# Attention outputs from stationary values and moving probabilities, two key groups in the two halves of a PSUM bank

## The chip, the core and the metric

The kernel runs on one core of a Trainium2 chip. A core has a matrix engine (TensorE, in the profile PE for matmuls and PEld for its weight loads), a vector engine (VectorE, DVE), an engine for pointwise functions (ScalarE, ACT), GpSimd (POOL) and a queue engine (SP) that here only issues transfers. Each works through its own instructions in a fixed order and waits on semaphores for the others. TensorE multiplies a stationary operand, loaded as weights, with a moving operand that streams past it, and writes into PSUM, whose banks hold 512 fp32 columns on 128 partitions. The metric is the time of one execution on the device in microseconds, the median of three runs. "Before" and "after" are the two versions of the kernel.

## What is computed

Two decoder layers on 256 tokens of width 2048. Each layer projects the normalised input into gating and attention parts, evaluates both, projects back, and adds a feed-forward part. The change is in the attention:

```python
q = rms_norm(q.reshape(b, nb, BLOCK, N_KV_HEADS, GROUP, HEAD_DIM), q_norm_g)   # 16 heads of 64
k = rms_norm(k.reshape(b, nb, BLOCK, N_KV_HEADS, HEAD_DIM), k_norm_g)          # 4 key groups
kb, vb = band(k), band(v)                    # previous and own block of 128 keys
scores = einsum('bnqkgd,bnskd->bnkgqs', q, kb) / sqrt(HEAD_DIM)
scores = where(valid, scores + bias, -1e30)  # causal window of 128 keys, bias per head and distance
probs = softmax(concatenate([scores, sink], -1), -1)[..., :-1]   # one extra logit per head
out_b = einsum('bnkgqs,bnskd->bnqkgd', probs, vb)
...
mixed = concatenate([rms_norm(out_a, out_norm_a), rms_norm(out_b, out_norm_b)], -1)
x = x + mixed @ w_out
x = x + (silu(h2 @ w_gate) * (h2 @ w_up)) @ w_down
```

All inputs and the output are float32. Four query heads share one key group. There are two query blocks of 128 tokens (t = 0 and 1); block 0 has 128 keys, block 1 has 256.

## The kernel before

**Units.** Every large product goes through weights of 256 x 512 fp32, one transfer each (`raw`). `split2` splits them into a high part `wh` (a cast on ScalarE, L99) and a low part `wl` (a subtraction on VectorE, L100), both fp32r; the activations are split the same way (`aT`, `hT`, with a high and a low half). `mm3` (L137 to L140) then makes three matmuls of 512 columns for one product. A unit is one such weight tile with its 12 large matmuls for the two token blocks (`unit`). Five buffers of `wh` and `wl` let the splits run ahead of TensorE by up to five units. In this text units are numbered from the start of a layer, and "behind unit n" is said of the place in TensorE's order.

**Order.** `later(delay, fn)` puts a step so many units ahead, and `tick` emits what is due after a unit. So the attention of a layer is strewn among the units of the input projection: `in_block(6)` (keys and values, units 0 to 7), `in_block(4)` and `in_block(5)` (queries), then four blocks for the gating part. The framework then fixes each engine's order, mostly as emitted, and picks free buffer slots.

**Attention.** `kv_norm` writes the projected keys and values to `zkv` and the normalised, transposed keys to `kT`; `q_norm` scales the queries per head (sum of squares, then a power -0.5 on GpSimd, L186) and transposes them to `qT`. For each key group g and query block t, `attend` computes the scores of four heads with 64-row matmuls, the even and odd heads on the two halves of the rows (L357, into `ps_s`); VectorE adds the bias (L365) and takes the maximum (L370); `nm` is its negative with the sink; ScalarE takes one exponential per head with the sum as a by-product (`den`, L378); VectorE makes `rden`, the reciprocal of the sum with the sink. Three units after `attend` comes `turn`: four transposes of probabilities on TensorE (L392) and a copy to `pt` (L393), twice for t = 1. Then `weigh`: for each head and key block one matmul with the 128 x 128 probabilities stationary and 64 columns of values moving (L399, into `ps_v`), and a multiplication by `rden` into `ob` (L408). When both blocks are done, `attend_end` sums the squares on ScalarE (L215), transposes the outputs (L208) and splits them with the gain of the norm into `pairs_b` (L198, L199). At the end `finish_rms` adds the partial sums to the norm's factor `rstd_b`, which `add_part` applies after the output projection.

**PSUM.** Eight banks: five for accumulators (`acc`), two (`dacc`), one (`sm`). `small_ps` hands them out in turn to the small products. The pool `spt` has four buffers for `s` and `pt`; the pool `big` has eight for `kT`, `qT`, `zkv`, `bias`, `wm` and others.

Of the kernel before, what the change touches and what calls it, by code (L numbers as in the profile page):

```python
# [12 lines left out]
F32 = mybir.dt.float32  # L13
# [3 lines left out]
ALU = mybir.AluOpType  # L17
# [28 lines left out]
)  # L46
ACTS = 6
HOLD = 2
VEC = 1.14
VEC_P = 0.6  # L50
MM = 0.227
# [16 lines left out]
def trunk(ctx, tc, x, xt, w_in, w_out, w_gate, w_up, w_down, sgu_w, sgu_g, consts,  # L68
# [49 lines left out]
    def later(delay, fn):  # L118
        pending.append((clock[0] + delay, next(serial), fn))
# [13 lines left out]
    def small_ps(shape, name):  # L133
        pool, tag = ((pm, "sm"), (pd, "dacc"), (pa, "acc"), (pd, "dacc"))[next(turns) % 4]
        return pool.tile(shape, F32, tag=tag, name=name)
# [33 lines left out]
        nc.tensor.matmul(heat, junk[:, :P], junk, start=i == 0, stop=i == WARM - 1)  # L169
    mhalf = cp.tile([P, 16], F32, tag="mhalf", name="mhalf")  # L170
    nc.vector.memset(mhalf, -0.5)
    tab = cp.tile([P, 16], F32, tag="tab", name="tab")
    nc.scalar.copy(tab, mhalf)
    ident = cp.tile([P, P], F32, tag="ident", name="ident")
# [2 lines left out]
    def small(shape, name):  # L177
        return sp.tile(shape, F32, tag=name, name=name)
# [15 lines left out]
    def split_gain(ps, lay, col, tag, spare=False):  # L194
        pair = pair_tile(tag, spare)
        for j in range(2):
            g = cst[:, lay, col + j : col + j + 1]
            nc.scalar.activation(pair[:, 0, j, :], ps[:, j, :], AF.Copy, scale=g)  # L198
            nc.vector.scalar_tensor_tensor(  # L199
                pair[:, 1, j, :], ps[:, j, :], g, f(pair[:, 0, j, :]), ALU.mult, ALU.subtract  # L200
            )
        return pair

    def transpose_pair(blocks, ps=None):
        ps = small_ps([P, 2, SEQ], "ps_t") if ps is None else ps
        for j in range(2):
            for t in range(NTOK):
                nc.tensor.transpose(  # L208
                    ps[:, j, t * P : (t + 1) * P], blocks[t][:, j * P : (j + 1) * P], ident
                )  # L210
        return ps

    def sum_sq(dst, src):
        void = zp.tile([P, NB], BF16, tag="z", name="void")
        nc.scalar.activation(void[:, : src.free_size()], src, AF.Square, accum_out=dst)  # L215
# [15 lines left out]
    def bc(a, n):  # L231
        return a.unsqueeze(2).to_broadcast([P, a.shape[1], n])
# [42 lines left out]
    for lay in range(L):  # L275
# [14 lines left out]
        def kv_norm(acc, lay=lay, layer=layer, zkv=zkv, kT=kT):  # L290
            kd = []
            zz = ap.tile([P, NTOK, NB], F32, tag="big", name="zkv", bufs=8)
            for t in range(NTOK):
                z = zz[:, t]
                nc.scalar.activation(z, acc[t], AF.Copy, scale=layer["rstd1"][t])
                zkv.append(z)
# [12 lines left out]

            for c in range(2):  # L310
                later(5 + c, lambda c=c: to_T(c))
# [22 lines left out]
            for c in range(2):  # L334
                later(5 + c, lambda c=c: to_T(c))

        ssb = [small([P, NKV], "ss4") for t in range(NTOK)]
        ob = {}
        bias = {}
        pairs_b = [None] * NKV  # L340

# [2 lines left out]
            nc.gpsimd.dma_start(bt, rdram[g * GRP : (g + 1) * GRP].rearrange("h q k -> q h k"))  # L344
            bias[g] = bt

        def attend(g, t, zkv=zkv, kT=kT, qT=qT, ob=ob, bias=bias, layer=layer):
            nkb = t + 1
            nk = nkb * P
            k0 = SEQ - nk  # L350
            nsink = layer["nsink"]
            s = ap.tile([P, GRP, nk], F32, tag="spt", name="s", bufs=4)
            halves = [small_ps([P, 2, nk], "ps_s") for r in range(2)]
            for i in range(2):
                for r in range(2):
                    h = g * GRP + 2 * i + r
                    nc.tensor.matmul(  # L357
                        halves[r][:, i, :],
                        qT[h // 8][HD * r : HD * r + HD, (h % 8) // 2, t * P : (t + 1) * P],
                        kT[HD * r : HD * r + HD, g, :nk],  # L360
                        start=True,
                        stop=True,
                    )
            for r in range(2):
                nc.vector.scalar_tensor_tensor(  # L365
                    s[:, r::2, :], halves[r], 1.0 / math.sqrt(HD), bias[g][:, r::2, k0:],
                    ALU.mult, ALU.add,
                )
            m = small([P, GRP], "m")
            nc.vector.tensor_reduce(m, s, AX.X, ALU.max)  # L370
            hs = slice(g * GRP, (g + 1) * GRP)
            nm = small([P, GRP], "nm")
            nc.vector.scalar_tensor_tensor(nm, m, -1.0, nsink[:, hs], ALU.mult, ALU.min)
            es = small([P, GRP], "es")
            nc.vector.tensor_tensor(es, nm, nsink[:, hs], ALU.subtract)
            den = small([P, GRP], "den")
            for i in range(GRP):
                nc.scalar.activation(  # L378
                    s[:, i, :], s[:, i, :], AF.Exp, bias=nm[:, i : i + 1],
                    accum_out=den[:, i : i + 1],  # L380
                )
            nc.scalar.activation(es, es, AF.Exp)
            rden = small([P, GRP], "rden")
            nc.vector.tensor_tensor(rden, den, es, ALU.add)
            nc.vector.reciprocal(rden, rden)
            pt = ap.tile([P, GRP * nkb, P], F32, tag="spt", name="pt", bufs=4)

            def turn(c):
                pst = small_ps([P, GRP, P], "ps_p")
                s4 = s.rearrange("p h (b k) -> p (h b) k", k=P)  # L390
                for i in range(GRP):
                    nc.tensor.transpose(pst[:, i, :], s4[:, c * GRP + i, :], ident)  # L392
                nc.vector.tensor_copy(pt[:, c * GRP : (c + 1) * GRP, :], pst)  # L393

            def weigh():
                pv = small_ps([P, GRP, HD], "ps_v")
                for i in range(GRP):
                    for b in range(nkb):
                        nc.tensor.matmul(  # L399
                            pv[:, i, :],  # L400
                            pt[:, i * nkb + b, :],
                            zkv[b][:, (NKV + g) * HD : (NKV + g + 1) * HD],
                            start=b == 0,
                            stop=b == nkb - 1,
                        )
                ob[g, t] = zp.tile([P, GRP * HD], F32, tag="z", name="ob")
                o3 = ob[g, t].rearrange("p (h d) -> p h d", d=HD)
                nc.vector.tensor_tensor(o3, pv, bc(rden, HD), ALU.mult)  # L408

            for c in range(nkb):  # L410
                later(3 + c, lambda c=c: turn(c))
            later(5 + t, weigh)

        def attend_end(g, lay=lay, ob=ob, ssb=ssb, pairs_b=pairs_b):
            for t in range(NTOK):
                sum_sq(ssb[t][:, g : g + 1], ob[g, t])
            ps = transpose_pair([ob[g, t] for t in range(NTOK)])
            pairs_b[g] = split_gain(ps, lay, C_GB + 2 * g, "aT", g >= 2)

        gate = {}  # L420

# [103 lines left out]
        acc = in_block(4)  # L525
        load_bias(0)
        q_norm(0, acc)
        for g in range(NKV):
            at = 6 + (27 * g) // 4
            later(at, lambda g=g: attend(g, 0))  # L530
            at += 2
            later(at, lambda g=g: attend(g, 1))
            if g + 1 < NKV:
                later(at, lambda g=g: load_bias(g + 1))
# [258 lines left out]
    return w.reshape(l, k // (4 * P), 2, 2, P, n // NB, NB).transpose(0, 5, 1, 3, 4, 2, 6)  # L793


def _cols(g):
    return g.reshape(-1, P).T

# [60 lines left out]
```

## Time and profile before

| | |
|---|---|
| Median of 3 runs | 1944.8 us (1944.8 to 1944.86) |
| Profiled execution | 1945.16 us, span of the trace 1943.5 us |
| TensorE busy | 1933.4 us, 99% of the span, 8894 matmul passes |
| VectorE, ScalarE, GpSimd busy | 1699.4 us (87%), 1151.3 us (59%), 127.1 us (7%) |
| Granted TensorE clock | 1.00 |

A row of the groups reads: line, engine, operation, output<-inputs, shape, count, then busy time and mean duration (ns) of one, then the engine's idle time before them and what ended it. A row of the timeline reads: start and duration in us, engine, line, operation, count; durations of matmuls overlap, so the distance of two starts is the price. A row of the waits reads: who waited for whom, microseconds in total, times, the longest. A plain fp32 matmul appears as two passes, a large fp32r one and a transpose as one.

### The profile page before, as it was taken

Reading aid. Unit: us, or ns where it says so; the run is one execution under the profiler, and the core shown is the slowest. Engines: PE = TensorE matmul, PEld = TensorE weight load, DVE = VectorE, ACT = ScalarE, POOL = GpSimd, SP = SyncE. Lnnn points to the kernel's source line nnn. Section 1 sums busy time; section 2 is a strip of 40 time slices with the busy share of each in tenths; the row PEclk is TensorE's granted clock in tenths of the full one; section 3 lists DMA queues with packets and bytes.
Section 4 is the critical chain, followed back from the end, with each engine's and each line's share of the span. In section 5 each row is a group of like instructions: output and inputs, shape, how many; then the busy total and the mean of one; then the engine's idle time right before and its main releaser. Section 6 shows DMA issues by size and latency. Waiting matters only on the chain.

```text
span 1943.5 us, 24615 instructions
## 1 busy us (share of the span) xinstructions
PE 1933.4 (99%) x8894; PEld 1588.5 (82%) x8894; DVE 1699.4 (87%) x1909; ACT 1151.3 (59%) x1455; POOL 127.1 (7%) x137
## 2 busy tenths in 40 slices
PE   9999999999999999999999999999999999999998
PEld 7788888888888888888888888888888888888887
DVE  6787689999999999999767876899999999999995
ACT  7465566666565665665555565666666566665662
POOL 1210001000000000000002100000000000000000
PEclk9999999999999999999999999999999999999999
DMA  8854557768668667767655445577677678768773
GB/s 322 266 174 152 184 170 233 223 226 266 216 215 268 219 229 246 221 226 247 206 194 191 158 163 182 176 247 219 222 243 234 215 244 240 237 217 245 240 239 120
DMA packets 119707, 424.43 MB, mean 218 GB/s; under 512 B 13168, under 2 KB 15344, under 8 KB 119584
## 3 DMA queue, kind: packets, MB, share of 16 engines
q1 hardware_dynamic: 106928, 377.57, 54.6%
q0 software_dynamic: 12512, 45.19, 12.5%
q8 instruction: 70, 1.15, 0.2%
q14 instruction: 53, 0.43, 0.1%
q10 hardware_dynamic: 144, 0.08, 0.0%
HBM read 420.66 MB, written 4.23 MB: 219 GB/s over the span
## 4 chain that ended last, share of the span: by engine, by line
PE 94%; DVE 3%; issue 1%; ACT 1%; DMA 1%; SPq 0%; ACTq 0%; DVEq 0%
PE m L140 11%; PE m L139 11%; PE m L138 11%; PE acc L138 10%; PE acc L140 10%; PE acc L139 10%; PE dacc L138 9%; PE dacc L139 9%; PE dacc L140 9%; DVE wl L100 2%; PE ps_v L399 1%; PE ps_f L208 1%; ACT wh L99 1%; PE ps_s L357 1%; PE ps_t L208 1%
## 5 line engine op out<-in xcount | busy, mean ns | idle before, releaser
L99 ACT CAST wh<-raw 128x1024 fp32r<-128x1024 f32 (+1 forms) x778 | 799.7, 1049 | 607.3 <-DVE raw L636 200.5
L100 DVE TENSOR_TENSOR wl<-raw,wh 128x1024 fp32r<-128x1024 f32 (+1 forms) x778 | 925.4, 1217 | 128.2 <-ACT wh L99 121.1
L138 PE MATMUL m<-wh,ext 128*128 128x512 f32 x576 | 225.7, 392 | 0.0
L138 PE MATMUL dacc<-wh,aT 128*128 128x512 f32 x576 | 225.0, 392 | 0.3
L139 PE MATMUL dacc<-wl,aT 128*128 128x512 f32 x576 | 225.1, 391 | 0.0
L139 PE MATMUL m<-wl,ext 128*128 128x512 f32 x576 | 224.6, 390 | 0.0
L140 PE MATMUL dacc<-wh,aT 128*128 128x512 f32 x576 | 224.5, 390 | 0.0
L140 PE MATMUL m<-wh,ext 128*128 128x512 f32 x576 | 224.3, 389 | 0.0
L100 DVE TENSOR_TENSOR wl<-t,wh 128x1024 fp32r<-128x1024 f32 x144 | 175.2, 1219 | 21.8 <-ACT wh L99 18.1
L99 ACT CAST wh<-t 128x1024 fp32r<-128x1024 f32 x144 | 151.4, 1052 | 57.5 <-PE dacc L140 40.0
L138 PE MATMUL acc<-wh,hT 128*128 128x512 f32 x448 | 180.3, 404 | 0.5 <-ACT wh L99 0.5
L139 PE MATMUL acc<-wl,hT 128*128 128x512 f32 x448 | 175.3, 391 | 0.8 <-DVE wl L100 0.7
L140 PE MATMUL acc<-wh,hT 128*128 128x512 f32 x448 | 175.3, 391 | 0.0
L138 PE MATMUL m<-wh,hT 128*128 128x512 f32 x432 | 168.5, 390 | 0.3 <-ACT wh L99 0.3
L140 PE MATMUL m<-wh,hT 128*128 128x512 f32 x432 | 168.1, 389 | 0.0
L139 PE MATMUL m<-wl,hT 128*128 128x512 f32 x432 | 168.1, 389 | 0.0
L138 PE MATMUL acc<-wh,aT 128*128 128x512 f32 x384 | 151.7, 395 | 0.0
L140 PE MATMUL acc<-wh,aT 128*128 128x512 f32 x384 | 149.9, 390 | 0.0
L139 PE MATMUL acc<-wl,aT 128*128 128x512 f32 x384 | 149.7, 390 | 0.0
L644 POOL DMA_DIRECT2D t<-in_w_gate_dram x72 | 61.5, 854 | 1327.3 <-DVE wl L100 828.5
L138 PEld LDWEIGHTS dacc<-wh,aT 128*128 128x128 f32 x576 | 108.1, 188 | 24.0 <-DVE xres L725 1.6
L139 PEld LDWEIGHTS dacc<-wl,aT 128*128 128x128 f32 x576 | 108.2, 188 | 23.9 <-DVE wl L100 2.2
(142 smaller groups left out, 2832.9 us busy)
## 6 DMA issues: line engine op xcount, KB each, us to landing
raw<-in_w_gate_dram SPq DMA_DIRECT2D x176, 512.0 KB, 5.3
raw<-in_w_up_dram SPq DMA_DIRECT2D x176, 512.0 KB, 4.5
raw<-in_w_down_dram SPq DMA_DIRECT2D x176, 512.0 KB, 4.9
raw<-in_w_in_dram SPq DMA_DIRECT2D x108, 512.0 KB, 4.3
t<-in_w_gate_dram POOLq DMA_DIRECT2D x72, 512.0 KB, 6.3
raw<-in_w_out_dram SPq DMA_DIRECT2D x64, 512.0 KB, 3.2
bias<-rdram POOLq DMA_DIRECT2D x8, 512.0 KB, 5.1
raw<-in_w_in_dram SPq DMA_DIRECT2D x8, 256.0 KB, 5.6
```

The source lines that it names most:

```text
L99: nc.scalar.copy(wh[:, j : j + step, :], src)
L100: nc.vector.tensor_tensor(wl[:, j : j + step, :], src, f(wh[:, j : j + step, :]), ALU.subtract)
L138: nc.tensor.matmul(acc, ah, wh, start=first, stop=False, **more)
L139: nc.tensor.matmul(acc, ah, wl, start=False, stop=False, **more)
L140: nc.tensor.matmul(acc, al, wh, start=False, stop=last, **more)
L208: nc.tensor.transpose(ps[:, j, t * P : (t + 1) * P], blocks[t][:, j * P : (j + 1) * P], ident)
L357: nc.tensor.matmul(halves[r][:, i, :], qT[h // 8][HD * r : HD * r + HD, (h % 8) // 2, t * P : (t + 1) * P], kT[HD * r : HD * r + HD, g, :n ...
L399: nc.tensor.matmul(pv[:, i, :], pt[:, i * nkb + b, :], zkv[b][:, (NKV + g) * HD : (NKV + g + 1) * HD], start=b == 0, stop=b == nkb - 1,)
L644: nc.gpsimd.dma_start(t2, w_gate[lay, b, i, 1], accum_op=ALU.add)
```

## The change

Two key groups (2G and 2G+1) and one query block now make one unit of attention (G, t) with eight heads, four per layer. The probabilities are scaled by `rden` on ScalarE right after the exponentials. `turn(b)` transposes one key block for both groups, eight transposes. In `weigh(b)` the values (64 columns, from `vhl`, a copy of the value half of `zkv`) are stationary and 512 columns of probabilities (four heads of 128 queries) move; the first group writes partitions 0 to 63 and the second 64 to 127 of the accumulator `ov`. So the outputs stand with the head's elements on the partitions, which is how the output projection takes them: they are not transposed any more. `leave` squares them, adds up over heads on VectorE, and splits them with the gain into `pairs_b`. `sum_b` adds over partitions with two small matmuls against a column of ones. The rows of `w_out` and the gain `out_norm_b` are reordered on the way in to match (`_paired`). `UNITS` says at which delay the four units come, `LAG` how many units later their first turn.

```diff
+LAG = {(0, 0): 4, (0, 1): 4, (1, 0): 4, (1, 1): 5}
+UNITS = {(0, 0): 6, (0, 1): 11, (1, 0): 19, (1, 1): 24}
...
-        zkv = []
+        vhl = ap.tile([P, NTOK, NKV * HD], F32, tag="big", name="vhl", bufs=8)
...
+                v = z[:, NKV * HD :]
+                nc.scalar.copy(vhl[:, t], v)
...
-        def attend(g, t, zkv=zkv, kT=kT, qT=qT, ob=ob, bias=bias, layer=layer):
+        def attend(G, t, kT=kT, qT=qT, vhl=vhl, ov=ov, bias=bias, layer=layer):
...
+            ss = []
+            for g in (2 * G, 2 * G + 1):
+                s = ap.tile([P, GRP, nk], F32, tag="spt", name="s", bufs=4)
+                halves = [small_ps([P, 2, nk], "ps_s") for r in range(2)]
...
+            for i in range(2 * GRP):
+                nc.scalar.activation(
+                    ss[i // GRP][:, i % GRP, :], ss[i // GRP][:, i % GRP, :], AF.Copy,
+                    scale=rden[:, i : i + 1],
+                )
+            pts = {}
+
+            def turn(b):
+                for k in range(2):
+                    pst = small_ps([P, GRP, P], "ps_p")
+                    for i in range(GRP):
+                        nc.tensor.transpose(pst[:, i, :], ss[k][:, i, b * P : (b + 1) * P], ident)
+                    pt = ap.tile([P, GRP * P], F32, tag="spt", name="pt", bufs=4)
+                    nc.vector.tensor_copy(pt, pst.rearrange("p h q -> p (h q)"))
+                    pts[b, k] = pt
+
+            def weigh(b):
+                if b == 0:
+                    ov[G, t] = pa.tile([P, GRP * P], F32, tag="acc", name="ov")
+                for k in range(2):
+                    g = 2 * G + k
+                    nc.tensor.matmul(
+                        ov[G, t][HD * k : HD * k + HD, :],
+                        vhl[:, b, g * HD : (g + 1) * HD],
+                        pts[b, k],
+                        start=b == 0,
+                        stop=b == nkb - 1,
+                        skip_group_check=True,
+                    )
+                if b == nkb - 1:
+                    leave(G, t)
+
+            for b in range(nkb):
+                later(LAG[G, t] + 3 * b, lambda b=b: turn(b))
+                later(LAG[G, t] + 2 + 3 * b, lambda b=b: weigh(b))
...
-        def attend_end(g, lay=lay, ob=ob, ssb=ssb, pairs_b=pairs_b):
...
+        def leave(G, t, lay=lay, ov=ov, sqs=sqs, pairs_b=pairs_b):
+            o = ov[G, t].rearrange("p (h q) -> p h q", q=P)
+            sq = zp.tile([P, GRP, P], F32, tag="z", name="sq")
+            nc.scalar.activation(sq, o, AF.Square)
+            nc.vector.tensor_reduce(
+                sqs[:, 2 * G + t, :], sq.rearrange("p h q -> p q h"), AX.X, ALU.add
+            )
+            for i in range(GRP):
...
+                nc.scalar.activation(dst[:, 0], o[:, i], AF.Copy, scale=g)
+                nc.vector.scalar_tensor_tensor(
+                    dst[:, 1], o[:, i], g, f(dst[:, 0]), ALU.mult, ALU.subtract
+                )
+
+        def sum_b(t, sqs=sqs):
+            ps = small_ps([P, 1], "ps_q")
+            for G in range(2):
+                nc.tensor.matmul(ps, sqs[:, 2 * G + t, :], ones, start=G == 0, stop=G == 1)
+            return inv_rms(ps, 1, SW)
...
-            later(at + 8, lambda g=g: attend_end(g))
+        later(1, lambda: load_bias(1))
+        for (G, t), at in UNITS.items():
+            later(at, lambda G=G, t=t: attend(G, t))
+        for g in (2, 3):
+            later(UNITS[0, 1] + g - 1, lambda g=g: load_bias(g))
...
-        rstd_b = [finish_rms(ssb[t], SW) for t in range(NTOK)]
+        rstd_b = [sum_b(t) for t in range(NTOK)]
```

More of the change, by code (lines that the diff above doesn't have):

```diff
@@ L171, in trunk @@
     nc.vector.memset(mhalf, -0.5)
+    ones = cp.tile([P, 1], F32, tag="ones", name="ones")
+    nc.vector.memset(ones, 1.0)
     tab = cp.tile([P, 16], F32, tag="tab", name="tab")
@@ L335, in q_norm @@
                 later(5 + c, lambda c=c: to_T(c))
-        ssb = [small([P, NKV], "ss4") for t in range(NTOK)]
-        ob = {}
+        ov = {}
+        sqs = zp.tile([P, 2 * NTOK, P], F32, tag="z", name="sqs")
         bias = {}
@@ L377, in attend @@
-            for i in range(GRP):
+            den = small([P, 2 * GRP], "den")
+            for i in range(2 * GRP):
                 nc.scalar.activation(
-                    s[:, i, :], s[:, i, :], AF.Exp, bias=nm[:, i : i + 1],
-                    accum_out=den[:, i : i + 1],
+                    ss[i // GRP][:, i % GRP, :], ss[i // GRP][:, i % GRP, :], AF.Exp,
+                    bias=nm[:, i : i + 1], accum_out=den[:, i : i + 1],
                 )
             nc.scalar.activation(es, es, AF.Exp)
-            rden = small([P, GRP], "rden")
+            rden = small([P, 2 * GRP], "rden")
@@ L384, in attend @@
             nc.vector.tensor_tensor(rden, den, es, ALU.add)
             nc.vector.reciprocal(rden, rden)
[L386 to L408, printed above, removed]
@@ L410, in attend @@
-            for c in range(nkb):
-                later(3 + c, lambda c=c: turn(c))
-            later(5 + t, weigh)
-        def attend_end(g, lay=lay, ob=ob, ssb=ssb, pairs_b=pairs_b):
[L415 to L418, printed above, removed]
+            for i in range(2 * GRP):
+                nc.scalar.activation(
+                    ss[i // GRP][:, i % GRP, :], ss[i // GRP][:, i % GRP, :], AF.Copy,
+                    scale=rden[:, i : i + 1],
+                )
@@ L813 @@
                     _cols(a["out_norm_a"][l]),
[L814 removed]
+                    _cols(_paired(a["out_norm_b"][l])),
                     a["sgu_b"][l].T,
```

64 lines of the change are left out of this document (32 added, 32 removed).

## The prediction

> **What bounds the kernel now.** I read the page first, then the waits of TensorE, then its stretches and its timeline around the attention.
>
> ```profile
> span 1943.5 us, 24615 instructions
> ...
> PE 1933.4 (99%) x8894; PEld 1588.5 (82%) x8894; DVE 1699.4 (87%) x1909; ACT 1151.3 (59%) x1455; POOL 127.1 (7%) x137
> ...
> PE 94%; DVE 3%; issue 1%; ACT 1%; DMA 1%; SPq 0%; ACTq 0%; DVEq 0%
> ```
> ```profile
> PE heat L169 <- DVE mhalf L171: 1.5, 1, 1.5
> PE acc L139 <- DVE wl L100: 0.7, 2, 0.5
> ```
> ```profile
> 1026.70:1174.90 148.20, 148.20 (x793) 122.65 (x792) 110.83 (x190) 84.70 (x170) 23.42 (x21) 1.00 0.51 173
> ```
>
> TensorE is busy 99% of the span, and the chain that ended last is 94% TensorE. The second fence is the waits of TensorE, longest first: the longest is at the start, the next 0.7 us in two pieces. The third is layer 1's attention stretch (busy us of PE, PEld, DVE, ACT, POOL, then clock): TensorE is busy all 148.2 us at full clock, VectorE 110.8 and ScalarE 84.7. So this kernel takes as long as the instructions on TensorE, one behind the other: a TensorE instruction removed shortens it at full price, one added lengthens it, and work elsewhere is free until TensorE must wait for it. Two sums are wanted: TensorE's time, and new waits.
>
> **The change on TensorE.** The timeline gives the price of each kind, as the distance between starts (the durations overlap):
>
> ```profile
> 37.81 1.03 PE L258 MATMUL ps_r<-oneh,relb 32*16 32x512 f32 x2
> 38.76 0.50 PE L138 MATMUL acc<-wh,hT 128*128 128x512 f32 x1
> ...
> 69.00 0.39 PE L139 MATMUL acc<-wl,hT 128*128 128x512 f32 x1
> ...
> 71.72 0.39 PE L139 MATMUL acc<-wl,hT 128*128 128x512 f32 x1
> ...
> 79.03 1.14 PE L357 MATMUL ps_s<-kT,qT 64*128 64x256 f32 x8
> 80.10 0.50 PE L138 MATMUL acc<-wh,hT 128*128 128x512 f32 x1
> 80.43 0.40 PE L139 MATMUL acc<-wl,hT 128*128 128x512 f32 x1
> ...
> 93.02 0.71 PE L357 MATMUL ps_s<-kT,qT 64*128 64x128 f32 x8
> 93.67 0.66 PE L392 MATMUL ps_p<-ident,s 128*128 128x128 f32 x4
> ...
> 109.53 0.60 PE L208 MATMUL ps_t<-ident,ob 128*128 128x128 f32 x4
> 109.88 0.48 PE L138 MATMUL acc<-wh,hT 128*128 128x512 f32 x1
> ...
> 123.54 1.89 PE L399 MATMUL ps_v<-zkv,pt 128*128 128x64 f32 x16
> 125.24 0.48 PE L138 MATMUL acc<-wh,hT 128*128 128x512 f32 x1
> 125.56 0.39 PE L139 MATMUL acc<-wl,hT 128*128 128x512 f32 x1
> ```
>
> - A unit of 12 large matmuls: 71.72 - 69.00 = 2.72 us, 0.227 each.
> - A plain fp32 matmul is two passes (x8 for 4 calls). A pass with 512 moving columns: (38.76 - 37.81) / 2 = 0.475, part of which is the change of shape; I take 0.44. By columns, 256 then cost 0.22.
> - Score group, 8 passes of 256 columns: 1.07 us, and the second large matmul behind it comes 0.33 instead of 0.227 later: 1.17. Eight passes one behind the other would be 1.76; so the two row halves (64 of 128 rows each) run side by side, 4 x 0.22 = 0.88, and 0.3 is for going into and out of halves. The group of 128 columns, 0.65 to the transposes behind it, says the same: 4 x 0.11 and 0.2 on the way in.
> - Weighted sum of one query block: 16 passes in 1.70, 0.106 each, and 0.09 behind.
> - Four transposes of outputs: 0.35 and 0.09 behind, 0.44.
>
> Removed over both layers: 192 passes L399 x 0.106 = 20.4, with some 0.7 behind the longer groups; 8 groups of output transposes x 0.44 = 3.5; score groups become 8 instead of 16 (two key groups back to back), so 8 entries into halves x 0.3 = 2.4; in layer 0 the first score group is scattered over three places among large matmuls that were late (the 0.7 above), now it stands after its inputs: about 1.3. Together 28.3. Score passes and the 96 transposes of probabilities stay as many.
>
> Added: 12 calls of weigh, each two matmuls (two passes) of 512 columns, into partitions 0-63 and 64-127 of one bank. The trace has no matmul in column halves. If the halves run side by side as the row halves do: 2 x 0.44 + 0.3 = 1.18, 14.2 in all. One behind the other: 4 x 0.44 + 0.3 = 2.06, 24.7. I take the first, the nearest row being L357, also two halves of the array in fp32. Then the sums of squares: 8 matmuls with a full stationary tile and one column, 16 passes at most 0.106 (the 64-column price), and entries: 2.0. Net on TensorE: -28.3 + 14.2 + 2.0 = **-12.1 us** side by side, -1.6 one behind the other.
>
> [...]
>
> ```profile
> L399 PEld LDWEIGHTS ps_v<-zkv,pt 128*128 128x128 f32 x192 | 23.6, 191 | 1.6 <-issue 0.7
> ```
>
> [...]
>
> **The change elsewhere.** In a layer ScalarE gains 32 scalings of probabilities (rden is applied before the product), 4 squares and 16 copies in leave, and loses 8 sums of squares and 8 copies: some 10 us against 63 idle (148.2 - 84.7). VectorE loses 8 scalings of ob and 8 subtractions, gains 4 reductions and 16 smaller subtractions: about even, with 37 us idle. That idle time hides these edits; where it doesn't lie at the right moment is the wait worked out below.
>
> ```profile
> bias<-rdram POOLq DMA_DIRECT2D x8, 512.0 KB, 5.1
> ```
>
> The bias loads are all issued ahead of the first scores now, before GpSimd's powers and the loads of wm, which need the slots of the first two biases; one landing takes 5.1 us, and the first use is some three units off. If they came late, the first L365 of a layer would wait a few us, and the scores' chain with it. The two products of sum_b stand five units behind the last weigh, when leave's few us are long over, and the first add_part needs their result four units later. The order of the feed-forward part is unchanged. All this is put at nothing.
>
> It waits at one place, I reckon. A unit (G, t) now does eight heads before its first turn, with LAG 4 against a delay of 3 for four heads. The tight one is (0,1), the first with 256 keys.
>
> ```profile
> L378 ACT ACTIVATE s<-s,nm 128x256 f32<-128x256 f32 x32 | 15.9, 498 | 3.6 <-DVE nm L373 3.6
> L215 ACT ACTIVATE void<-ob 128x256 bf16<-128x256 f32 x16 | 6.6, 410 | 5.2 <-DVE ob L408 5.2
> L99 ACT CAST wh<-raw 128x1024 fp32r<-128x1024 f32 x774 | 797.3, 1051 | 605.9 <-DVE raw L636 200.5 <-PE acc L140 160.8 <-PE dacc L140 65.9
> ```
> ```profile
> L365 DVE SCALAR_TENSOR_TENSOR s<-ps_s,bias 128x512 f32<-128x512 f32 x16 | 10.5, 682 | 0.9 <-PE ps_s L357 0.9
> L370 DVE TENSOR_REDUCE m<-s 128x4 f32<-128x1024 f32 x8 | 9.7, 1211 | 0.0
> L100 DVE TENSOR_TENSOR wl<-raw,wh 128x1024 fp32r<-128x1024 f32 x774 | 922.7, 1219 | 128.0 <-ACT wh L99 120.9
> ```
> ```profile
> 85.35 0.51 ACT L378 ACTIVATE s<-s,nm 128x256 f32<-128x256 f32 x1 [1.11 <-DVE nm L373]
> ...
> 85.86 0.50 ACT L378 ACTIVATE s<-s,nm 128x256 f32<-128x256 f32 x1
> ```
> ```profile
> 1053.15 0.16 DVE L184 TENSOR_SCALAR ms<-hs 128x8 f32<-128x8 f32 x1
> ...
> 1055.98 0.69 DVE L324 TENSOR_TENSOR zq<-zq,ir 128x512 f32<-128x512 f32 x1 [1.46 <-POOL ir L186]
> ```
>
> Count from the start of its scores, S. TensorE reaches the turn after 2.05 of scores (16 passes of 256: 8 x 0.22 + 0.3), 4 units of 2.72, one weigh 1.18 and two groups of transposes 0.88: S + 15.0; six transposes further, S + 15.6. VectorE in its built order: shortly before S stand the second head norm's ms and, 2.3 to 2.8 us later, zq's multiplication (the last fence has 2.83; GpSimd computes the power between), so it is free at S + 2.5 to 3. Then four weight splits wl among four L365, two L370 and nm; back to back these run about 0.07 under their durations: 4 x 1.15 + 4 x 0.62 + 2 x 1.15 + 0.16 = 9.5, nm at S + 12.3. ScalarE: eight exponentials 0.5 apart (85.35 to 85.86), 4.0; es and one copy of leave 0.5; a weight cast 1.05 that stands ahead of the scalings; six scalings of 0.31 (0.41 by L215, less 0.1 of overlap): 1.9. That is S + 19.7 against S + 15.6: 4.1 us of waiting, 3.0 to 3.5 if the power comes in 2.3; I take 3.7. Layer 1 has the same order there: **7.4 us** in all. Queued behind the waiting transposes are the large matmuls of unit 31; on ScalarE, behind the exponentials that wait for nm, stand the casts from unit 33 on, and units 28 to 32 are cast before. So TensorE has its weights when it goes on, and nothing follows. Units (0,0) and (1,0) have 128 keys and 0.5 to 1 us to spare, (1,1) has LAG 5 and next to nothing.
>
> **The sum.** The profiled execution took 1945.16 us (span 1943.5 and 1.7 around it), 0.36 above the median 1944.8. -12.1 + 7.4 = -4.7: 1940.5 in a profile, **1940.1** as a median. Measurement of this kernel can tell about 0.2%, 3.9 us, from no change.
>
> **Rivals.**
> - *No wait.* GpSimd answers early and the scalings are shorter than L215: -12.1 less a microsecond or two: 1934. For it: TensorE never waited 1 us in the attention before. Against it: the delay grew by a unit and the work doubled.
> - *Halves one behind the other* (the slower side). No column half is in the trace. Place: the 12 weigh calls; price 0.88 each over the forecast, 10.5; TensorE then reaches the turn 0.9 later, so the waits are 2.8 each. -1.6 + 5.6 = +4.0: 1949. It decides the sign from about 1.6 us per weigh on. For it: both halves take different moving columns through all rows, which L357 does not.
> - *Weight loads in the open.* If the four loads of a weigh, 0.19 each by L399, are not hidden: 12 x 0.76 = 9.1, less 1.5 of shorter waits: -12.1 + 9.1 + 5.9 = +2.9: 1948. Against it: 16 passes in 1.70. [...]
> - *ScalarE late in all four units.* If the exponentials and scalings cost full durations (0.69 with the accumulator's read, 0.41), (0,1) waits 6 us, (1,1) 2, the others 0.5: 9 a layer. -12.1 + 18 = +6: 1951. The same rows against it: 85.35 to 85.86.
>
> ```profile
> 1.52 4.34 PE L169 MATMUL heat<-junk 128*128 128x512 bf16 x12 [1.52 <-DVE mhalf L171]
> ```
>
> - *The clock drops in the waits.* At the start, 12 matmuls of 512 columns took 4.34 us where 12 x 0.227 are 2.72: some 1.6 lost after idling. Twice that: -4.7 + 3.2: 1943. [...]
>
> **How the numbers follow.** Forecast (waits 4 to 10 us in all): 0.47. No wait: 0.14. One behind the other: 0.17. Loads in the open: 0.05. ScalarE late: 0.12. Clock: 0.05. Faster: 0.33 of the forecast's share (waits under 8 us) and no wait, 0.47. Slower: ScalarE late, and half of the two cases about 1948 to 1949, with 0.22 in all. Same: the rest, 0.31. The range, 1933 to 1950, reaches from no wait to one behind the other and leaves out most of ScalarE late; the likeliest case alone has 1936 to 1943.
>
> **What would show it.** Right: TensorE's waits name s (or the scalings) before ps_p, about 3.7 us once a layer at the first turn of (0,1); ov's four passes start in two pairs 0.44 apart; no waits elsewhere over 1 us; the feed-forward stretch as long as before. Wrong: ov's passes start in four steps of 0.44; waits at other turns; a granted clock under 1.00; large matmuls waiting for wh or wl.

## The result, and the profile after

The changed kernel took 1949.6 us (median of 10 runs, 1948.06 to 1953.05) against 1944.8 (10 runs, 1943.93 to 1945.05): 1.0028 times as long, 95% interval 1.002 to 1.0036. It is slower by 4.8 us where 4.7 less was forecast. The profiled run took 1949.08.

The page of the changed kernel, its first lines and the chain that ended last:

```profile
span 1947.3 us, 24324 instructions
...
PE 1931.8 (99%) x8734; PEld 1572.1 (81%) x8734; DVE 1700.0 (87%) x1882; ACT 1171.3 (60%) x1507; POOL 128.8 (7%) x137
...
PE 88%; DVE 6%; ACT 2%; issue 2%; POOL 1%; DMA 0%; ACTq 0%; SPq 0%; POOLq 0%; DVEq 0%
```

TensorE's share of the chain fell from 94 to 88%, VectorE's doubled: waits have come into the path. Waits of TensorE (us in all, times, longest), and then those of its weight loads, which are counted apart and cover pauses between transposes:

```profile
PE ps_p L406 <- ACT s L396: 4.5, 2, 2.9
PE heat L171 <- DVE mhalf L173: 1.5, 1, 1.5
PE acc L141 <- DVE wl L102: 1.0, 2, 0.6
PE ps_s L364 <- DVE pt L408: 0.9, 2, 0.5
```
```profile
PEld ps_p L406 <- ACT s L396: 12.6, 29, 3.3
```

Transposes wait for ScalarE's scalings (L396) now, and scores (L364) for VectorE's copy pt. The stretches of the two attentions (busy us of PE, PEld, DVE, ACT, POOL, then the granted clock):

```profile
58.00:210.00 152.00, 148.44 (x719) 114.53 (x718) 113.43 (x178) 95.22 (x196) 22.59 (x21) 0.99 0.53 190
1027.00:1179.00 152.00, 147.91 (x713) 114.01 (x712) 111.41 (x175) 94.00 (x193) 24.45 (x20) 0.99 0.49 166
```

TensorE is idle 3.6 and 4.1 us of these, and its clock is no longer 1.00. Where it fell:

```profile
106.00:109.60 3.60, 3.53 (x11) 2.77 (x11) 1.99 (x4) 3.58 (x8) 0.00 (x0) 0.53 0.37 140
1075.40:1079.00 3.60, 3.60 (x10) 2.61 (x11) 2.66 (x4) 3.58 (x8) 0.00 (x0) 0.53 0.51 163
```

In both layers the clock stood at half for 3.413 us (the trace's record of it), from within the first turn of (0,1) on.

**The places.** TensorE in layer 0, around the turns of (0,1), the scores of (1,0) and the first turn of (1,1); the large matmuls between are left out:

```profile
87.23 2.00 PE L364 MATMUL ps_s<-kT,qT 64*128 64x256 f32 x16
92.15 1.08 PE L416 MATMUL ov<-pt,vhl 128*64 128x512 f32 x4
...
104.12 2.48 PE L406 MATMUL ps_p<-ident,s 128*128 128x128 f32 x6 [1.55 <-ACT s L396]
...
121.25 0.93 PE L364 MATMUL ps_s<-kT,qT 64*128 64x128 f32 x10
122.70 0.71 PE L364 MATMUL ps_s<-kT,qT 64*128 64x128 f32 x6 [0.52 <-DVE pt L408]
...
158.26 3.13 PE L406 MATMUL ps_p<-ident,s 128*128 128x128 f32 x8
...
1073.78 2.88 PE L406 MATMUL ps_p<-ident,s 128*128 128x128 f32 x7 [2.91 <-ACT s L396]
```

The last row is (0,1) in layer 1. Eight transposes that nothing holds up take 1.03. Six here take 2.48 after 1.55 of idling, eight take 3.13 at (1,1): they start 0.40 apart, and so do ScalarE's scalings.

From the starts of the large matmuls the attention of a layer can be measured: from the first one of unit 18 of the layer (the first kv and q blocks are behind it) to the first of unit 60. In the table, all in us, is the length of that stretch; further kernels are added below:

| kernel | layer 0 | layer 1 | both |
|---|---|---|---|
| before | 150.8 | 148.3 | 299.1 |
| changed | 152.1 | 152.2 | 304.2 |

Taking from each unit its 2.72 and the price of its groups where they do not wait (0.93 for a turn, 1.18 for (1,0)'s scores) leaves what was lost:

| place in the changed kernel | forecast, a layer | layer 0 | layer 1 |
|---|---|---|---|
| first turn of (0,1) and the unit behind it | 3.7 | 4.9 | 6.2 |
| of this, half clock for 3.413 us | 0 | 1.7 | 1.7 |
| scores of (1,0), bank not yet copied out | 0 | 1.1 | 1.0 |
| first turn of (1,1) | 0 | 2.1 | 2.1 |

17.4 us are lost. Without them the stretch would be 286.8, 12.3 under before, where the prediction had 12.1 for TensorE's instructions. These are the profiled runs: start, feed-forward part and end together became 1.2 us shorter (3.9 between the profiled runs, 5.1 in the attention).

### The profile page after: what moved, and what is told of

It is laid out like the page before. It is cut to its first block, busy times and chain, and to the rows that moved or that the text cites. A ratio compares the mean times of both kernels' runs of the same rounds, so it can differ in the third digit from the quotient of the medians.

```text
span 1947.3 us, 24324 instructions
## 1 busy us (share of the span) xinstructions
PE 1931.8 (99%) x8734; PEld 1572.1 (81%) x8734; DVE 1700.0 (87%) x1882; ACT 1171.3 (60%) x1507; POOL 128.8 (7%) x137
## 3 DMA queue, kind: packets, MB, share of 16 engines
q0 software_dynamic: 12512, 45.19, 12.3%
## 4 chain that ended last, share of the span: by engine, by line
PE 88%; DVE 6%; ACT 2%; issue 2%; POOL 1%; DMA 0%; ACTq 0%; SPq 0%; POOLq 0%; DVEq 0%
PE m L142 11%; PE m L141 11%; PE m L140 11%; PE dacc L140 9%; PE dacc L141 9%; PE dacc L142 9%; PE acc L140 8%; PE acc L141 8%; PE acc L142 8%; DVE wl L102 2%; POOL ir L190 1%; ACT wh L101 1%; PE ps_f L212 1%; ACT s L387 1%; ACT s L396 1%
```

## The experiments

**Theory** (A in the expectations; A2 and A3 add what later rounds showed): TensorE's instructions became as much shorter as forecast, and ScalarE's scalings, late at the turns, gave it back, with a half clock behind. **Rivals**: the new instructions are dearer (B); VectorE bounds the stretch whatever is moved (C and E); the clock falls for another reason (D); the bank that leave holds is the true releaser (F).

**Later turns.** The first edit (e1) gives the turns of both 256-key units more time, the second (e2) leaves (1,1) at 5.

```
-LAG = {(0, 0): 4, (0, 1): 4, (1, 0): 4, (1, 1): 5}
-UNITS = {(0, 0): 6, (0, 1): 11, (1, 0): 19, (1, 1): 24}
+LAG = {(0, 0): 4, (0, 1): 6, (1, 0): 4, (1, 1): 6}
+UNITS = {(0, 0): 6, (0, 1): 11, (1, 0): 22, (1, 1): 27}
```

> The two 256-key units get their first turn later: LAG of (0,1) from 4 to 6 units, of (1,1) from 5 to 6, and the units of G = 1 begin three units of weights later (22 and 27), which also takes (1,0)'s scores away from the turn ahead of them. Nothing else changes; every instruction stays. Theory A (TensorE's own instructions became about 12 us shorter, as predicted, and waits of TensorE for ScalarE and the half clock that follows them gave it back, some 16 us in the attention): no wait over 1 us at a turn, granted clock 1.000, about 1933 us. Rival B (the new instructions are dearer than reckoned, the waits only show slack): 1946 to 1950, the large matmuls or the groups longer in the trace. Rival C (VectorE is the bound of the attention, so a later turn waits as long): waits of 2 to 5 us at the same turns, about 1948.

> As the kernel with both turns later, but LAG of (1,1) stays at 5. Theory A, with a wait of its own at (1,1) as the trace has it (two of 2.1 us): about 1937 us, waits of about 2 us once a layer at the first turn of (1,1). If the wait at (1,1) was only carried on from the late (0,1): 1933, no wait there. Rival B: 1946 to 1950.

Measured: 1950.75 (ratio to before 1.0036, 1.0023 to 1.0048) and 1951.15 (1.0037, 1.0025 to 1.005). The forecast of 16 us of gain was wrong. The profile of the first was taken in a run of 1954.38; waits of TensorE in it:

```profile
PE acc L141 <- DVE wl L102: 7.8, 5, 3.3
PE ps_p L406 <- DVE aT L446: 5.7, 2, 3.1
```

The scalings are no longer named. The turn of (0,1) now waits for a PSUM bank: the accumulator of (0,0) is emptied by leave, and its first copy and last subtraction stand far apart:

```profile
94.18 0.36 ACT L445 ACTIVATE aT<-ov,cst 128x128 fp32r<-128x128 f32 x1
...
110.58 0.35 DVE L446 SCALAR_TENSOR_TENSOR aT<-ov,cst,aT 128x128 fp32r<-128x128 f32 x1
```

The bank is held for 17 us. And large matmuls wait for wl behind (1,1)'s scores. The clock stood at half for 20.5 us of this run (granted clock 0.994), not for 6.8 as in the changed kernel (0.998). The second edit has the same waits (7.9 and 6.7 us). So the scalings were one of several late things.

**The clock.** Dummy matmuls in the idle time at (0,1), in the changed kernel (two more ahead of each of the first six transposes are left out here):

```
+                warm = (G, t, b) == (0, 1, 0)
+                if warm:
...
+                    for i in range(14):
+                        nc.tensor.matmul(at, junk[:, :P], junk, start=True, stop=True)
...
```

> The changed kernel with dummy bf16 matmuls on the identity (256 columns each) in the idle time at the first turn of (0,1): 14 ahead of the first transpose (1.6 us) and two ahead of each of the first six transposes; they write into the bank of the second group of transposes ahead of these. LAG, waits and everything else stay. Theory A with the clock as a part of its own: the wait stays about as long, the clock stays at 1.000 instead of falling to half for 3.4 us in each layer, and 2 x 1.7 = 3.4 us are saved: about 1946 us. Rival D (the clock falls for another reason than idling): clock 0.998 or less, 1949 to 1951.

Measured: 1951.02 (1.0034, 1.0021 to 1.0046). Two stretches of layer 0:

```profile
100.00:112.00 12.00, 11.14 (x64) 8.26 (x63) 8.22 (x14) 11.97 (x31) 1.09 (x1) 1.00 0.55 169
120.00:128.00 8.00, 6.40 (x31) 4.72 (x30) 7.07 (x13) 1.05 (x1) 1.68 (x2) 0.82 0.50 165
```

With TensorE kept working the clock stays up at (0,1) in both layers, 1.00 from 100 to 112 us in layer 0 and 0.999 over the run with the one half clock below, so its cause is shown and rival D falls. The price is not: the time was to fall to 1946 and did not. Here, in layer 0, all eight transposes stand ahead of the next large matmul, not six, so TensorE goes on with it at 107.66 us, not at 106.25; and the scores then wait 3.2 us for pt instead of 0.9 (both layers together), with a half clock of their own at (1,0) in layer 0.

The price can be read in the changed kernel. At the end of the half stretch in layer 1 the large matmuls start 0.43 apart, at full clock 0.227:

```profile
1077.94 0.63 PE L140 MATMUL acc<-wh,hT 128*128 128x512 f32 x1
1078.37 0.63 PE L141 MATMUL acc<-wl,hT 128*128 128x512 f32 x1
```

So while large matmuls are there to be done, nearly half of the stretch is lost, up to 1.7 us of 3.413. The runs of one kernel fit that. Those of the kernel with leave's copies first and later turns (e11, below), by granted clock: 1942.85 at 1.000; 1944.04, 1944.24, 1945.2 and 1945.93 at 0.999; 1946.08 at 0.998; 1947.24, 1947.71, 1948.13 and 1948.57 at 0.997; 1948.25 at 0.996. A clock lower by 0.003 is 0.003 x 1945 = 5.8 us of full clock lost, and the four runs at 0.997 are 5.1 us longer by their mean than the one at 1.000. By themselves these runs don't settle the price, since a run with longer waits would show a lower clock too. The changed kernel's runs follow the same line, 1948.06 to 1949.63 at 0.998 and 1952.61 and 1953.05 at 0.995.

**The scalings and the place of (1,0).** Three edits: the scalings left out; the units of G = 1 one unit later; both.

```
-            for i in range(2 * GRP):
-                nc.scalar.activation(..., AF.Copy, scale=rden[:, i : i + 1])
```
```
-UNITS = {(0, 0): 6, (0, 1): 11, (1, 0): 19, (1, 1): 24}
+UNITS = {(0, 0): 6, (0, 1): 11, (1, 0): 20, (1, 1): 25}
```

> The changed kernel without ScalarE's 64 scalings of the probabilities (the probabilities are then not divided by their sum; the sum is still formed). LAG and the order of units stay. Theory A with ScalarE's chain as what is late: the turns then wait for the exponentials alone, 8 x 0.41 = 3.3 us earlier; the wait at (0,1) falls from 3.0 and 4.8 to under 1 us, the one at (1,1) from 2.1 to nothing, the clock stays at 1.000: about 1937 us. Rival C (VectorE's scores and maxima come too late, the scalings hide behind them): waits of 2 us or more stay at (0,1), 1944 or more.

> The changed kernel with its scalings on ScalarE, and the units of G = 1 begun one unit of weights later (20 and 25). Theory A2: the wait of (1,0)'s scores for the copy pt (2.2 us in both layers) goes, the waits at the first turns of (0,1) and (1,1) stay with the half clock behind (0,1): about 1947 us. Rival E: 1949 to 1951.

> The kernel without the 64 scalings (the probabilities stay undivided), with the units of G = 1 begun one unit of weights later (20 and 25 instead of 19 and 24), so that (1,0)'s scores stand two units behind the turn before them instead of one. Theory A2 (TensorE's instructions are 12.4 us shorter; given back by waits behind two in-order queues: ScalarE's, where the scalings and leave's copies stand behind the exponentials, and VectorE's, where the copies pt that free the scores' banks stand behind other work): with the scalings gone and the banks copied in time, neither wait is left, the clock stays at 1.000: 1933 to 1935 us, no wait of TensorE over 1 us. Rival E (whatever is saved at one place is given back at the next, since VectorE as a whole is the bound of the stretch): 1942 to 1944 again, with the wait at another place.

Measured: 1943.07 (0.999, 0.9981 to 0.9999), 1950.52 (1.0028, 1.0018 to 1.0038) and 1935.91 (0.9955, 0.9941 to 0.9968). Waits of TensorE without the scalings, and then with both edits:

```profile
PE ps_s L364 <- DVE pt L403: 5.2, 5, 1.7
```
```profile
PE ps_s L364 <- DVE pt L403: 1.1, 2, 0.7
```

Without the scalings TensorE gains 3.9 us at (0,1) in layer 0 and 6.1 in layer 1. It so reaches (1,0)'s scores earlier and waits there for VectorE's copy pt: with the half clock behind that wait, 3.6 and 3.9 are given back four units on. The 1943.07 lies between the forecasts of theory A (1937) and rival C (1944 or more). The shift alone gives nothing, as rival E had it: the scores' wait is gone, but large matmuls wait 5.2 us for wl (1.0 before), and the clock is halved four times, not twice (0.996 over the run, 0.998 before the shift). Together the edits give 13.7 us against the changed kernel, just short of theory A2's 1933 to 1935 and far from rival E's 1942 to 1944; one wait over 1 us is left, 1.2 us of a large matmul for a subtraction of leave. The two losses stand one behind the other, so each edit alone shows only what the other lets through.

**Who scales.** With the units at 20 and 25, two multiplications of a whole key group on another engine in place of the eight scalings, here on VectorE (on GpSimd the same line with `nc.gpsimd`):

```
+            for k, s in enumerate(ss):
+                nc.vector.tensor_tensor(s, s, bc(rden[:, k * GRP : (k + 1) * GRP], nk), ALU.mult)
```

> As the kernel begun one unit later, but the 64 scalings on ScalarE are 16 multiplications on VectorE of one key group each (s by rden, 128x512 or 128x1024); everything is computed. By the wl rows 128x1024 costs VectorE 1.2 us, so 2.4 for the unit (0,1) against 3.3 of ScalarE behind a cast of 1.05. Theory A2: the first turn of (0,1) gets its first transposes 2 us earlier and its last 1.8 earlier, its wait falls from 3 to 5 us to 1 to 2; (1,1) waits under 1 us; the clock stays at 1.000 in most runs: 1936 to 1941 us, ahead of the kernel before. Rival E: VectorE has 2.4 us more of work a unit, its copies and weight splits come later, 1947 to 1952.

> As the kernel with the scalings on VectorE, but those 16 multiplications on GpSimd, which is busy 7% of the span (its affine select of 128x1024 took 1.1 to 1.4 us). Theory A2, if GpSimd multiplies at about that pace and its waits for the loads of wm do not stand ahead: 1935 to 1940 us. If it is slower by half or more, or waits for a load of wm ahead of them (up to 4.6 us in the trace): the wait at (0,1) stays at 3 us or more, and with it the half clock: 1947 to 1955.

Measured: 1947.62 on VectorE (1.0012, 1.0003 to 1.0021), 1964.44 on GpSimd (1.0099, 1.0086 to 1.0113). Both are later than theory A2 had them, the first where rival E had it, the second outside every forecast. The groups, first on VectorE, then on GpSimd:

```profile
L396 DVE TENSOR_TENSOR s<-s,rden 128x1024 f32<-128x1024 f32 x8 | 11.2, 1439 | 0.0
...
L442 ACT ACTIVATE aT<-ov,cst 128x128 fp32r<-128x128 f32 x32 | 11.6, 362 | 5.7 <-DVE aT L443 5.5
```
```profile
L396 POOL TENSOR_TENSOR s<-s,rden 128x1024 f32<-128x1024 f32 x8 | 18.9, 2379 | 43.6 <-DVE rden L394 43.6
```

GpSimd took 2.4 us for a key group, not 1.1 to 1.4; TensorE waited 19.2 us for it. Its 2379 ns are 1.65 times VectorE's 1439 here and 1.95 times its 1219 in a later run (e12).

On VectorE, (1,1)'s turn no longer waits over 1 us, but (0,1)'s still does (7.2 us in four waits). The row of L442 tells why: ScalarE's copies of leave wait 5.5 us for VectorE's subtractions. Each copy waits for the subtraction before it, so the bank stays held for four round trips through two busy queues.

**Leave's order.** Copies first, in the changed kernel alone (e13) and with units 20 and 25 (e10):

```
             for i in range(GRP):
                 ...
                 nc.scalar.activation(dst[:, 0], o[:, i], AF.Copy, scale=g)
-                nc.vector.scalar_tensor_tensor(...)
+                todo.append((dst, o[:, i], g))
+            for dst, src, g in todo:
+                nc.vector.scalar_tensor_tensor(...)
```

> The changed kernel with leave's copies first and nothing else changed (LAG 4, 4, 4, 5; units at 6, 11, 19, 24). Theory A3: the waits at the turns of (0,1) and (1,1) for the scalings and of (1,0)'s scores for pt stay, a little shorter: 1947 to 1949. Rival F: about 1942.

> As the changed kernel with the units of G = 1 begun one unit later (20, 25), and leave issues its four copies on ScalarE first and its four subtractions on VectorE behind them, instead of one by one; same operations. In the trace each copy of leave waits for the subtraction before it, so the accumulator of (0,0) is read in four round trips through two busy queues, for 15 us, and its bank is wanted by a turn of (0,1). LAG stays at 4 and 5. Theory A3 (three things are late at the turns: ScalarE's scalings, the bank held by leave, the copies pt): the bank comes free 10 us earlier, but at LAG 4 the scalings are still late: waits of 2 to 4 us at the first turn of (0,1) and 2 at (1,1) stay, with the half clock: 1945 to 1949. Rival F (the bank was the true releaser and the scalings only the name in the trace): no wait at (0,1), about 1940.

Measured: 1951.02 (1.0034, 1.0021 to 1.0047) and 1946.86 (1.0009, 1.0 to 1.0017). The group of copies in the changed kernel, and with the new order:

```profile
L445 ACT ACTIVATE aT<-ov,cst 128x128 fp32r<-128x128 f32 x32 | 11.6, 361 | 7.6 <-DVE aT L446 7.6
```
```profile
L446 ACT ACTIVATE aT<-ov,cst 128x128 fp32r<-128x128 f32 x32 | 9.1, 374 | 0.0
```

The round trips are gone: from the first copy to the last subtraction of (0,0) in layer 0 it is 7.5 us instead of 16.7. But at LAG 4 the scalings are still late (ps_p waited 6.1 us for them in both). Rival F falls: the bank was not the only releaser. Alone, the new order gives nothing; with the units at 20 and 25 it is worth 3.7 us (1950.52 without it).

**All together.** Leave's copies first and LAG 5 and 6, units 21 and 26, with the scalings on ScalarE (e11), on VectorE (e12) and left out (e16).

> Leave's copies first, and later turns: LAG of (0,1) 5, of (1,1) 6, the units of G = 1 begun at 21 and 26. Everything is computed, with the scalings on ScalarE. Theory A3: the turn of (0,1) comes 2.7 us later and its bank is free, so its wait falls to 0 to 1.5 us, (1,1) doesn't wait, the clock stays at 1.000: 1933 to 1938 us, ahead of the kernel before by 0.35 to 0.6%. Rival E (VectorE bounds the stretch as a whole): 1945 or more. Rival B (later turns alone, as with LAG 6 and 6, give nothing): 1949 to 1951.

> As the kernel with leave's copies first and later turns, with the scalings on VectorE (16 multiplications of one key group) instead of ScalarE. Theory A3: no wait over 1 us, clock 1.000, 1933 to 1937 us, the same as with ScalarE or up to 2 us less. Rival E: VectorE's 13 us a layer more of work show as waits for wl or pt: 1940 or more.

> Leave's copies first and later turns (units at 6, 11, 21, 26; LAG 4, 5, 4, 6), with the 64 scalings left out (the probabilities stay undivided): the floor of the two kernels that differ from it only in where the scalings run. By TensorE's own instructions, 12.4 us under the kernel before: 1932 to 1934 us; at most one wait over 1 us. If the waits of scores for pt stay without the scalings: 1935 to 1937.

Measured: 1946.08 (1.0006, 0.9997 to 1.0015), 1940.91 (0.9976, 0.9966 to 0.9986), 1933.6 (0.9941, 0.9929 to 0.9954). Waits of TensorE in these three, in this order:

```profile
PE acc L141 <- DVE wl L102: 6.8, 4, 2.9
```
```profile
PE ps_p L403 <- DVE s L396: 2.4, 3, 1.6
PE ps_s L364 <- DVE pt L405: 1.7, 2, 0.9
```
```profile
PE heat L171 <- DVE mhalf L173: 1.5, 1, 1.5
PE acc L141 <- DVE wl L102: 1.2, 2, 0.6
```

The last is the floor: no new wait over 1 us, 11.2 us under before, the clock at 1.000. That is TensorE's sum on the chip, and rival B falls. With VectorE scaling, 1940.91 is rival E's number (1940 or more) and not the forecast 1933 to 1937. With ScalarE scaling, the forecast of 1933 to 1938 was wrong too: at (1,1) four weight splits stand on VectorE behind the scores, the maxima and leave's subtractions, and TensorE waits for wl.

Two last placings of the version on VectorE: LAG 6 for (0,1) with units 22 and 27 (e14), and scores two units behind the turn before them, units 12, 22 and 28 (e15).

> As the kernel with leave's copies first, later turns and the scalings on VectorE, with LAG of (0,1) 6 instead of 5 and the units of G = 1 begun at 22 and 27 instead of 21 and 26. If the rest of the waits is a matter of place: the turn of (0,1) waits no more (1.0 and 2.4 us less), 1937 to 1938 us. If VectorE's work as a whole bounds the stretch: 1940 to 1942, the waits at other places.

> As the kernel with leave's copies first, later turns and the scalings on VectorE, but the scores of (0,1) and of (1,1) stand two units behind the turn before them instead of one (units at 6, 12, 22, 28; LAG 4, 5, 4, 5), so that VectorE has copied pt and their banks are free. Place: no wait of scores for pt (1.7 us less) and the turn of (0,1) as late as with LAG 6: 1936 to 1938 us. VectorE as the bound: 1940 to 1942.

Measured: **1938.88** (0.9969, 0.9957 to 0.9981) and 1939.47 (0.9972, 0.9961 to 0.9982). Both compute everything and beat both kernels; both lie between the two forecasts, place (up to 1938) and VectorE as the bound (1940 or more). The first, page and waits:

```profile
PE 1925.3 (99%) x8734; PEld 1570.9 (81%) x8734; DVE 1712.3 (88%) x1898; ACT 1150.2 (59%) x1443; POOL 128.8 (7%) x137
...
PE 91%; DVE 5%; issue 1%; ACT 1%; POOL 1%; DMA 1%; SPq 0%; ACTq 0%; POOLq 0%; DVEq 0%
```
```profile
PE heat L171 <- DVE mhalf L173: 1.5, 1, 1.5
PE ov L413 <- DVE pt L405: 1.3, 2, 0.9
```

Place gave 2 us of the 7 above the floor. Of the 5 that remain, the weigh of (0,1) has most: it waits for pt, 2.0 and 1.4 us over its 1.1. The stretches, in us, as in the table above:

| kernel | layer 0 | layer 1 | both |
|---|---|---|---|
| scalings left out, units 20 and 25 (e6) | 147.6 | 144.1 | 291.7 |
| scalings on VectorE (e12) | 147.1 | 146.9 | 294.0 |
| the same, LAG 6 (e14) | 146.6 | 146.3 | 292.8 |
| floor, scalings left out (e16) | 144.2 | 143.7 | 287.9 |

Rival E was nearest by number in four runs (e7, e8, e11, e12), yet it holds only in part. VectorE as a whole is not the bound: e6 and e16 go faster with the same VectorE work as the changed kernel, and in e14 VectorE is busy for 120.3 of the 147 us from 58 to 205 and for 117.0 of the 146 from 1022 to 1168. But the waits that are left name VectorE: what it queues ahead of pt, s and wl comes late. That this alone makes the last 5 us was not tested.

## Why the prediction was wrong

- **TensorE's sum: right.** -12.1 was forecast; -12.3 remains in the trace when the waits are taken out, and -11.2 was measured in the floor kernel.
- **Halves side by side: right.** One weigh and what stands behind it, in layer 1:

```profile
1082.96 0.39 PE L142 MATMUL acc<-wh,hT 128*128 128x512 f32 x1
1083.28 1.08 PE L416 MATMUL ov<-pt,vhl 128*64 128x512 f32 x4
1084.29 0.50 PE L140 MATMUL acc<-wh,hT 128*128 128x512 f32 x1
1084.62 0.39 PE L141 MATMUL acc<-wl,hT 128*128 128x512 f32 x1
```

  1084.62 - 1082.96 = 1.66, less two steps of 0.227: 1.2, forecast 1.18. The four passes of the weigh at 92.15 begin at 92.147, 92.153, 92.627 and 92.633: two pairs, 0.48 apart. One behind the other (2.06), and loads in the open (0.76 more than 1.18), fall.
- **The wait at (0,1): right in place and cause, in size by some luck.** Without the clock 3.2 and 4.5 us, forecast 3.7. Its chain in layer 0, and the group of these scalings:

```profile
98.06 0.16 DVE L382 SCALAR_TENSOR_TENSOR nm<-m,nsink 128x8 f32<-128x8 f32 x1
```
```profile
98.31 0.51 ACT L387 ACTIVATE s<-s,nm 128x256 f32<-128x256 f32 x1 [4.19 <-DVE nm L382]
...
102.62 1.03 ACT L101 CAST wh<-raw 128x1024 fp32r<-128x1024 f32 x1
103.56 3.31 ACT L396 ACTIVATE s<-s,rden 128x256 f32<-128x256 f32 x8
```
```profile
L396 ACT ACTIVATE s<-s,rden 128x256 f32<-128x256 f32 x32 | 13.2, 498 | 0.0
```

  With S = 87.23, nm is done at S + 11.0 (forecast 12.3), but the scalings start 0.40 apart and not 0.31. The overlap of 0.1 was right; the row was not: a scaling lasts 0.498, while L215, without a scale of its own for each partition, lasts 0.41. The kernel before has a nearer row, L198, a copy with such a scale: 0.471. So in layer 0 two errors cancel. And layer 1 has not "the same order": there zq's multiplication starts 4.9 us after S, not 1.0, nm is done at S + 12.3, and the wait is 1.3 us longer.
- **"(1,1) has LAG 5 and next to nothing": wrong, 2.1 us in each layer.** Its chain:

```profile
148.37 1.28 ACT L387 ACT_TABLE_LOAD   x1 [0.61 <-DVE nm L382]
...
153.62 0.20 ACT L391 ACTIVATE es<-es 128x8 f32<-128x8 f32 x1
...
157.70 3.30 ACT L396 ACTIVATE s<-s,rden 128x256 f32<-128x256 f32 x8
```

  A table load of 1.28 stands ahead of the exponentials, and es is ready at 153.8 but VectorE comes to rden's sum only later, behind the gate's v and two weight splits:

```profile
156.98 0.16 DVE L393 TENSOR_TENSOR rden<-den,es 128x8 f32<-128x8 f32 x1
```

  ScalarE itself then stands idle for 2.4 us, for a copy of leave that waits for a subtraction in the same queue of VectorE. The prediction put this wait at nothing and followed the chain for (0,1) alone, where none of this stands in it.
- **"Units (0,0) and (1,0) have 128 keys and 0.5 to 1 us to spare": the turns had, the scores not.** It counted when data are ready and never when PSUM banks come free: 1.1 and 1.0 us at (1,0)'s scores, which it had at nothing.
- **The clock: wrong, up to 3.4 us.** It stood as a rival at 0.05, and the forecast's sum had nothing for it. The price, 1.6 a pause, was right (up to 1.7); that it would happen was not believed.

In sum: the step that failed is "It waits at one place", with (1,1), the bank at (1,0)'s scores and the clock put at nothing. -4.7, + 3.4 for two half clocks, + 4.2 at (1,1), + 2.1 for the bank, makes + 5.0. With - 0.2 for TensorE's sum, + 0.3 at (0,1) and - 1.2 outside the attention it is the + 3.9 between the profiled runs; that + 5.0 stands so near to the + 4.8 between the medians is luck. The rival that came nearest, ScalarE late in all four units, had 9 us a layer, as measured (8.7), with other parts: its scalings of 0.41 and its 2 us at (1,1) are right, but the exponentials start 0.49 apart and not 0.69, and it has neither the clock nor the bank. Rival "no wait" falls.

## What to carry to other kernels

When a change removes work from the bounding engine and makes each dependent step larger, follow every unit's chain through each in-order queue, and list for each instruction both its data and the PSUM bank that it writes: who empties that bank, and what is queued ahead of that. A wait taken away uncovers the next one, so try edits in pairs before one is called useless; here later turns and leave's order gave nothing alone, VectorE's scalings (with the units one later) 2 us, and the three together 10.7. An evacuation that alternates between two engines held its bank here for four round trips (16.7 us, 7.5 with the copies first): let the engine that reads first read everything.

## What was not expected of the hardware

- The clock fell here behind a wait of 1.55 us, and once behind none over 0.15. In layer 0 TensorE was idle for 1.55 us and then made transposes 0.40 us apart; the clock was halved from 106.07 to 109.48. In layer 1 it was idle for 2.91. In e11 the clock was halved at 108.29 behind eight transposes with no pause over 0.15 us (first row); with short pauses but quicker transposes (e12, four in 0.63 us) it stayed up, 1.000 over that run:

```profile
105.47 3.27 PE L406 MATMUL ps_p<-ident,s 128*128 128x128 f32 x8
105.87 0.63 PE L403 MATMUL ps_p<-ident,s 128*128 128x128 f32 x4 [0.26 <-DVE s L396]
107.01 0.63 PE L403 MATMUL ps_p<-ident,s 128*128 128x128 f32 x4 [0.51 <-DVE s L396]
```

- In the changed kernel's record the clock fell once in each attention, each time for 3.413 us. The stretches at full clock before these, 98.99 us from the start of the record and 965.97 us, are 29.0 and 283.0 times as long. In the 3.41 us before 106.07 TensorE was busy for 1.64 us, with five transposes, and the clock was halved next; in the 3.41 us up to 160.68, at (1,1), it was busy for 2.99, and the clock stayed at 1.00:

```profile
102.66:106.07 3.41, 1.64 (x5) 0.69 (x5) 2.60 (x6) 3.41 (x9) 1.34 (x1) 1.00 0.59 204
106.07:109.48 3.41, 3.36 (x10) 2.65 (x11) 1.80 (x4) 3.39 (x7) 0.00 (x0) 0.50 0.38 147
157.27:160.68 3.41, 2.99 (x12) 1.36 (x10) 2.28 (x5) 3.24 (x9) 0.00 (x0) 1.00 0.80 284
160.00:164.00 4.00, 3.79 (x17) 2.71 (x17) 3.22 (x6) 4.00 (x8) 0.00 (x0) 1.00 0.36 133
```

  How little work it takes for the clock to fall is not shown.
